# Gates of a block: first two outputs interleaved, six PSUM buffers, later dhid loads, sums and norm rows tied behind products

## The chip, the cores and the metric

The kernel runs on one core of one Trainium2 chip. The metric is the device time of one execution in microseconds, the median of several runs.

## The reference, cut to what matters

One inference step of a decoder trunk (one layer, D_MODEL 1024, D_FF 2816): 1024 prompt tokens and 8 x 4 sample tokens, 1056 columns in all. Two mixers and an output projection come first; the change lies behind them, in the last two lines of the layer and the end of the feed-forward part:

```
up = rmsnorm(x, g_ffn) @ w_up;  conv = causal depthwise conv of up, width 3, with a carried buffer
a, v = split(conv);             f = (gelu(a) * v) @ w_down        # the hidden row is called dhid below
x = x + f
x = x + sigmoid(rmsnorm(x, g_ple) @ w_ple_gate) * (p @ w_ple_proj)
return x, ..., new_buf           # new_buf: the last up rows, outputs conv_prompt and conv_sample
```

## The kernel before, in words

Every float32 product is made from operands split into a high part (an ACT cast to fp32r) and a low part (a subtraction on DVE or POOL): `split`, lines 82 and 83. `mm3` (L85 to L88) issues three matmuls for one product: high x high, high x low, low x high.

The program's tail works on columns. The 1056 columns are three blocks of 352. In a block, eight **down outputs** of 128 channels are summed over the 22 tiles of the hidden row dhid (66 matmuls each, six weight groups of up to four tiles, in PSUM buffers "pd"); then eight **gate outputs** are summed over the eight tiles of the new x (24 matmuls each, two weight groups, PSUM buffers "pu").

- **Down output** (`down_out`): DVE adds the PSUM result to x (`xb`), ACT scales it into gg (high), DVE makes gg's low part, ACT squares it, and POOL, for the last output DVE, adds the square to `sqb`. The gate products read all eight gg.
- **Sums and rows**: `sums` contracts sqb with ones on TensorE (three matmuls), DVE makes the reciprocal root in some twelve tiny steps (L99 to L113); `rows` transposes it on TensorE (L2217) and DVE copies it to `rb` (L2218).
- **rest(o)**: y = gate sum x rb (DVE), sigmoid (ACT), x pe (DVE), + xb (DVE). **out_turn(o)** transposes y on TensorE (L2241), ACT copies and stores it.
- **Weights**: w_down and w_ple_gate tiles and the blocks of dhid come through one ring of five buffers `raw`, loaded by SP in a fixed sequence (`raw_load`, `pull`, L1648 to L1664): the next load is recorded when a buffer has been consumed. Weight groups are split three groups ahead into four buffers `wx` (`dn_unit`, `ahead`), odd groups on DVE and even ones on POOL, the cast always on ACT.
- **dhid**: the next block's hidden rows, eight pieces h(0) to h(7) of up to three tiles (528 KB), are loaded into the same ring (`hid_raw`) and split (`hid_split`, tiles M) during the gates of the block before. Block 0's are split during the last up-projection pair (`last_pair`).
- **Conv rows**: `last_rows` transposes the last up rows LU (eight groups of four transposes, L2136); ACT copies and stores them. They run from the list `side`.

A scheduler at build time puts the recorded instructions of each engine into one order; each engine then works in that order and waits at semaphores. `tc.issue_after(ins)` adds to an instruction that it may not stand before `ins` on its own engine; it issues nothing. The order in which the eight gate outputs and their dhid pieces are recorded is the loop at L2254:

```
for o in range(8):
    pgs[o] = gate(o)
    if b < 2:
        hid_split(b + 1, o, V)
```

Of the kernel before, what the change touches and what calls it, by code (L numbers as in the profile page):

```python
# [21 lines left out]
BLK = T // 3  # L22
# [33 lines left out]
def body(tc, I, O):  # L56
# [8 lines left out]
    with ctx:  # L65
# [19 lines left out]
        def mm3(out, lh, ll, rh, rl, start, stop_):  # L85
            PE.matmul(out, lh, rh, start=start, stop=False)  # L86
            PE.matmul(out, lh, rl, start=False, stop=False)  # L87
            PE.matmul(out, ll, rh, start=False, stop=stop_)  # L88

# [1606 lines left out]
        for b in range(3):  # L1696
            kgs = [(o, kg) for o in range(8) for kg in range(6)]
            if b == 0:
                kgs = [(o, kg) for q in (range(4), (4, 5)) for o in range(2) for kg in q] + kgs[12:]
            units += [("d", o, kg) for o, kg in kgs] + [("g", o, kg) for o in range(8) for kg in range(2)]  # L1700

        for b in range(3):
# [9 lines left out]
            for o in range(8):  # L1712
                raw_load(("g", o), k8(), w_pg[:, :, cols_(o)])
                if b < 2:
                    hid_raw(b + 1, o)

# [387 lines left out]
        def last_pair(m):  # L2104
            if m in ORDER[:6]:
                g = ORDER.index(m)
                hid_split(0, g, V if g % 2 else G)
            if m == 4:
                hid_split(0, 6, V)
# [3 lines left out]
        while post:  # L2113
            step()
        hid_split(0, 7, V)
        pX.close()
# [16 lines left out]
        def last_rows(q):  # L2133
            pt = ps.tile([128, 512], F32, name="pt")
            for j in range(4):
                PE.transpose(pt[:18, j * 128:(j + 1) * 128], LU[:, q + j], ident)  # L2136
            lo_ = p2.tile([18, 512], F32, name="lo_", bufs=1)
            A.copy(lo_, pt[:18])
            A.dma_start(cvp[:, q * 128:(q + 4) * 128], lo_[0:2])
            A.dma_start(cvs[:, q * 128:(q + 4) * 128], lo_[2:18])  # L2140

        side = [lambda q=q: last_rows(q) for q in range(0, NH2, 4)]

        def block(b):
# [10 lines left out]
            def p_in(o):  # L2155
                pe[o] = btile("pe", 3)
                SP.dma_start(pe[o], dpp[cols_(o), c])

            def down_group(pd, kg):
                wt = wq.pop(0)  # L2160
                ahead()
                for k in range(4 * kg, min(4 * kg + 4, NH)):
                    mm3(pd, wt[:, 0, k % 4], wt[:, 1, k % 4], hp_[k][0], hp_[k][1], k == 0, k == NH - 1)

# [27 lines left out]
            if b == 0:  # L2192
                for kgs in (range(4), (4, 5)):
                    for o in range(2):
                        down(o, kgs)
            for o in range(2 if b == 0 else 0, 8):
                down(o, range(6))
                for _ in range(3):
                    if side:
                        side.pop(0)()  # L2200

# [17 lines left out]

            def gate(o):  # L2220
                pg_ = psu.tile([128, BLK], F32, name="pu")
                for kg in range(2):
                    wt = wq.pop(0)
                    ahead()
                    for k in range(4 * kg, 4 * kg + 4):
                        mm3(pg_, wt[:, 0, k % 4], wt[:, 1, k % 4], GG[k][:, 0], GG[k][:, 1], k == 0, k == 7)
                return pg_

            def rest(o, pg_):
                y = Y[o] = btile("y", 3)  # L2230
                V.tensor_tensor(y, pg_, rb, OP.mult)
# [18 lines left out]

            pgs = {}
            p_in(0)
            p_in(1)
            for o in range(8):  # L2254
                pgs[o] = gate(o)
                if b < 2:
                    hid_split(b + 1, o, V)
                if o == 0:
                    rst = sums()
                    continue  # L2260
                if o == 1:
                    rows(rst)
                    rest(0, pgs.pop(0))
                rest(o, pgs.pop(o))
                if o < 7:
                    p_in(o + 1)
                out_turn(o - 1)
            out_turn(7)
# [44 lines left out]
```

## Time and profile before

| | |
|---|---|
| runs | 2036.23, 2048.02, 2044.82 us, median 2044.82 |
| profiled execution | 2045.7 us, its span 2043.8 us |
| TensorE busy | 1947.7 us, 95% of the span |
| VectorE (DVE), ScalarE (ACT), GpSimd (POOL) busy | 1247.0, 915.6, 878.2 us |
| mean granted TensorE clock | 0.974 |
| the tail that the change touches | from some 1640 us to the end |

The span is that of the profiled execution on its core; the execution's own time has 1.9 us around it. A busy share is an average over stages: in the down products TensorE is busy almost all of the time, in the gates less. What a change in the gates is worth is read from the waits there.

### The profile page before, as it was taken

What the parts mean: (1) busy time and instruction counts of PE and PEld (TensorE: products, weight loads), DVE (VectorE), ACT (ScalarE), POOL (GpSimd) and SP (SyncE); (2) the same over time, 40 slices, a digit from 0 to 9 for tenths busy, and PEclk for the clock granted to TensorE, in tenths of its full rate; (3) what the DMA queues carried; (4) which work ended last, traced back from release to release, by engine and by line L of the source; (5) the groups of instructions that cost most, each with busy time, mean ns of one, the idle gap of its engine ahead of it and who ended that gap; (6) DMA issues with size and microseconds to landing.
All of it is one profiled execution on the core that took longest, in us unless ns stands there. A gap on an engine that the chain in (4) does not pass through costs nothing.

```text
span 2043.8 us, 35840 instructions
## 1 busy us (share of the span) xinstructions
PE 1947.7 (95%) x13329; PEld 1832.4 (90%) x13329; DVE 1247.0 (61%) x2451; ACT 915.6 (45%) x1910; POOL 878.2 (43%) x934
## 2 busy tenths in 40 slices
PE   7998999999999989999999899999999999899998
PEld 6897888888787778888999899999999989899998
DVE  5518533245778856665554877878888872734524
ACT  5512332243566634555333454444444454544543
POOL 1106441102314212222432777878788854344342
PEclk9998999999999969999999999999999999999999
DMA  7402221244322100004465422222222274755743
GB/s 242 137 11 65 67 62 51 69 124 137 87 58 58 32 1 12 2 1 151 132 179 183 130 98 90 69 81 77 72 87 66 92 234 136 229 176 175 224 143 99
DMA packets 291927, 211.53 MB, mean 103 GB/s; under 512 B 38417, under 2 KB 273092, under 8 KB 291754
## 3 DMA queue, kind: packets, MB, share of 16 engines
q1 hardware_dynamic: 275102, 195.86, 32.2%
q10 hardware_dynamic: 16652, 13.39, 2.1%
q8 instruction: 105, 1.72, 0.4%
q14 instruction: 68, 0.56, 0.1%
HBM read 161.07 MB, written 46.78 MB: 102 GB/s over the span
## 4 chain that ended last, share of the span: by engine, by line
PE 73%; DVE 10%; POOL 2%; ACT 2%; DMA 2%; issue 2%; SPq 1%; ACTq 0%; DVEq 0%; POOLq 0%
PE q L2023 21%; PE pd L87 4%; PE pd L86 4%; PE pd L88 4%; PE q L1950 3%; PE pm L88 3%; PE pm L87 3%; PE pm L86 3%; PE pv L1382 3%; PE pt L86 2%; PE pt L87 2%; PE pt L88 2%; PE p L86 2%; PE p L88 2%; PE p L87 1%
## 5 line engine op out<-in xcount | busy, mean ns | idle before, releaser
L2023 PE MATMUL q<-M,wx 128*128 128x264 f32 x2112 | 280.8, 286 | 2.0 <-DVE up L2043 2.0
L2023 PEld LDWEIGHTS q<-M,wx 128*128 128x128 f32 x2112 | 268.1, 189 | 2.3 <-issue 2.1
L83 POOL TENSOR_TENSOR wx<-raw,wx 128x512 fp32r<-128x512 f32 x108 | 146.3, 1356 | 228.2 <-ACT wx L82 222.0
L82 ACT CAST wx<-raw 128x512 fp32r<-128x512 f32 x226 | 133.4, 597 | 194.9 <-PE pd L88 114.4
L2023 PE MATMUL q<-P,wx 128*128 128x264 f32 x1584 | 216.2, 286 | 0.1
L2023 PEld LDWEIGHTS q<-P,wx 128*128 128x128 f32 x1584 | 200.6, 188 | 3.8 <-DVE up L2035 3.8
L83 DVE TENSOR_TENSOR wx<-raw,wx 128x512 fp32r<-128x512 f32 (+1 forms) x118 | 91.4, 776 | 141.6 <-ACT wx L82 138.2
L86 PE MATMUL pd<-M,wx 128*128 128x352 f32 x528 | 171.6, 325 | 0.0
L88 PE MATMUL pd<-M,wx 128*128 128x352 f32 x528 | 171.1, 324 | 0.0
L87 PE MATMUL pd<-M,wx 128*128 128x352 f32 x528 | 171.1, 324 | 0.0
L2066 DVE SCALAR_TENSOR_TENSOR cv<-up,cw,cv 128x1024 f32<-128x1024 f32 x88 | 143.2, 1627 | 28.3 <-ACT cv L2058 28.3
L88 PE MATMUL pm<-xh,wl 128*128 128x352 f32 x384 | 127.0, 331 | 0.0
L87 PE MATMUL pm<-xl,wh 128*128 128x352 f32 x384 | 126.5, 329 | 0.0
L86 PE MATMUL pm<-xh,wh 128*128 128x352 f32 x384 | 126.4, 329 | 0.0
L1756 ACT CAST wx<-raw 128x512 fp32r<-128x512 f32 x110 | 67.9, 618 | 71.9 <-PE q L2023 47.1
L86 PEld LDWEIGHTS pd<-M,wx 128*128 128x128 f32 x528 | 99.8, 189 | 0.1
L87 PEld LDWEIGHTS pd<-M,wx 128*128 128x128 f32 x528 | 99.7, 189 | 0.0
L88 PEld LDWEIGHTS pd<-M,wx 128*128 128x128 f32 x528 | 99.6, 189 | 0.1
L1364 POOL TENSOR_TENSOR Pt<-Pt,mstT 128x128 f32<-128x128 f32 x64 | 30.8, 484 | 160.1 <-ACT Pt L1363 160.1
L1950 PE MATMUL q<-M,wx 128*128 128x264 f32 x720 | 92.0, 289 | 4.1 <-POOL wx L83 2.6
L1950 PEld LDWEIGHTS q<-M,wx 128*128 128x128 f32 x720 | 89.8, 191 | 5.3 <-POOL wx L83 3.1
L83 POOL TENSOR_TENSOR wl<-wst,wh 128x1024 fp32r<-128x1024 f32 x16 | 39.3, 2456 | 104.2 <-ACT wh L82 100.1
(706 smaller groups left out, 5480.6 us busy)
## 6 DMA issues: line engine op xcount, KB each, us to landing
raw<-w_down SPq DMA_DIRECT2D x48, 512.0 KB
raw<-w_up SPq DMA_DIRECT2D x44, 512.0 KB
raw<-w_ple_gate SPq DMA_DIRECT2D x24, 512.0 KB
dhid<-cv SPq DMA_DIRECT2D x22, 528.0 KB
raw<-dhid SPq DMA_DIRECT2D x21, 528.0 KB
raw<-w_down SPq DMA_DIRECT2D x24, 384.0 KB
wst<-w_in SPq DMA_DIRECT2D x16, 512.0 KB
cb<-cache_ckv SPq DMA_DIRECT2D x64, 128.0 KB
```

The source lines that it names most:

```text
L82: A.copy(hi, src)
L83: (eng or G).tensor_tensor(lo, src, hi.bitcast(F32), OP.subtract)
L86: PE.matmul(out, lh, rh, start=start, stop=False)
L87: PE.matmul(out, lh, rl, start=False, stop=False)
L88: PE.matmul(out, ll, rh, start=False, stop=stop_)
L1364: masked[0] = G.tensor_tensor(Pt[:, :128], Pt[:, :128], mstT, OP.add)
L1382: PE.matmul(W["pv"][:, j, :DV + 1], Pts[k][:, q0:q0 + 128], Vb[hp][:, k, e], start=k == 0, stop=k == i)
L1756: A.copy(w[:, 0], s)
L1950: PE.matmul(p_[:, n, :QW], a_, b_[:, k % 4], start=k + x == 0 and kg == 0, stop=k == 7 and x == 2)
L2023: PE.matmul(o_, l_, r_, start=start and k + x == 0, stop=k + x == 5, skip_group_check=not start)
L2066: V.scalar_tensor_tensor(C[:, :S], U[:, tp:tp + S], w[tp], C[:, :S], op0=OP.mult, op1=OP.add)
```

## The change

In words: (1) `mm3` returns its last matmul, so that others can be tied behind it. (2) The first two gate outputs are computed together, weight group by weight group. (3) Gate outputs 3 to 5 use the three "pd" buffers, which makes six PSUM buffers. (4) h(0) is loaded behind g(3), h(1) to h(3) behind g(4) to g(6), h(4) to h(7) behind g(7); the splits of the pieces are recorded from gate 3 on. (5) `sums` is tied behind the first two outputs (48 matmuls), `rows` behind the third (72). (6) The transposes of outputs are recorded later and left to the scheduler. (7) The conv rows run two per down output behind its products, with two copies' buffers, not three before them. (8) The last piece of block 0's dhid is split behind the first four groups of outputs 0 and 1. (9) "pe" and "y" have four buffers.

```diff
@@ -85,7 +85,7 @@
         def mm3(out, lh, ll, rh, rl, start, stop_):
             PE.matmul(out, lh, rh, start=start, stop=False)
             PE.matmul(out, lh, rl, start=False, stop=False)
-            PE.matmul(out, ll, rh, start=False, stop=stop_)
+            return PE.matmul(out, ll, rh, start=False, stop=stop_)
 
         def mm2(out, l2, rh, rl, start, stop_):
 
@@ -1697,7 +1697,7 @@
             kgs = [(o, kg) for o in range(8) for kg in range(6)]
             if b == 0:
                 kgs = [(o, kg) for q in (range(4), (4, 5)) for o in range(2) for kg in q] + kgs[12:]
-            units += [("d", o, kg) for o, kg in kgs] + [("g", o, kg) for o in range(8) for kg in range(2)]
+            units += [("d", o, kg) for o, kg in kgs] + [("g", o, kg) for op in ((0, 1), (2,), (3,), (4,), (5,), (6,), (7,)) for kg in range(2) for o in op]
 
         for b in range(3):
             if b == 0:
@@ -1711,8 +1711,9 @@
                     dn_load(o, i)
             for o in range(8):
                 raw_load(("g", o), k8(), w_pg[:, :, cols_(o)])
-                if b < 2:
-                    hid_raw(b + 1, o)
+                for g in {7: (4, 5, 6, 7)}.get(o, (o - 3,) if o > 2 else ()):
+                    if b < 2:
+                        hid_raw(b + 1, g)
 
         wsum = {}
 
@@ -2105,14 +2106,13 @@
             if m in ORDER[:6]:
                 g = ORDER.index(m)
                 hid_split(0, g, V if g % 2 else G)
-            if m == 4:
+            if m == 3:
                 hid_split(0, 6, V)
 
         for j in range(NH):
             up_pair(j, first_pair if j == 0 else last_pair if j == NH - 1 else lambda m: None)
         while post:
             step()
-        hid_split(0, 7, V)
         pX.close()
         f1.close()
 
@@ -2134,12 +2134,14 @@
             pt = ps.tile([128, 512], F32, name="pt")
             for j in range(4):
                 PE.transpose(pt[:18, j * 128:(j + 1) * 128], LU[:, q + j], ident)
-            lo_ = p2.tile([18, 512], F32, name="lo_", bufs=1)
+            lo_ = p2.tile([18, 512], F32, name="lo_", bufs=2)
             A.copy(lo_, pt[:18])
             A.dma_start(cvp[:, q * 128:(q + 4) * 128], lo_[0:2])
             A.dma_start(cvs[:, q * 128:(q + 4) * 128], lo_[2:18])
 
         side = [lambda q=q: last_rows(q) for q in range(0, NH2, 4)]
+
+        pe_ = [None]
 
         def block(b):
             c0 = b * BLK
@@ -2153,14 +2155,14 @@
                 SP.dma_start(xb[o], dx2[cols_(o), c])
 
             def p_in(o):
-                pe[o] = btile("pe", 3)
+                pe[o] = btile("pe", 4)
                 SP.dma_start(pe[o], dpp[cols_(o), c])
 
             def down_group(pd, kg):
                 wt = wq.pop(0)
                 ahead()
                 for k in range(4 * kg, min(4 * kg + 4, NH)):
-                    mm3(pd, wt[:, 0, k % 4], wt[:, 1, k % 4], hp_[k][0], hp_[k][1], k == 0, k == NH - 1)
+                    pe_[0] = mm3(pd, wt[:, 0, k % 4], wt[:, 1, k % 4], hp_[k][0], hp_[k][1], k == 0, k == NH - 1)
 
             def down_out(o, pd):
                 V.tensor_tensor(xb[o], pd, xb[o], OP.add)
@@ -2193,11 +2195,14 @@
                 for kgs in (range(4), (4, 5)):
                     for o in range(2):
                         down(o, kgs)
+                    if 0 in kgs:
+                        hid_split(0, 7, V)
             for o in range(2 if b == 0 else 0, 8):
                 down(o, range(6))
-                for _ in range(3):
+                for _ in range(2):
                     if side:
-                        side.pop(0)()
+                        with tc.issue_after(pe_[0].ins):
+                            side.pop(0)()
 
             def sums():
                 pss = ps.tile([128, 512], F32, name="pt")
@@ -2217,17 +2222,25 @@
                     PE.transpose(pt[:, t0:t0 + n], rst[:n, i:i + 1].to_broadcast([n, 128]), ident[:n, :n])
                 V.tensor_copy(rb, pt[:, :BLK])
 
-            def gate(o):
-                pg_ = psu.tile([128, BLK], F32, name="pu")
+            pgs = {}
+
+            def gate(os_):
+                for o in os_:
+                    pgs[o] = psd.tile([128, BLK], F32, name="pd") if 2 < o < 6 else psu.tile([128, BLK], F32, name="pu")
                 for kg in range(2):
-                    wt = wq.pop(0)
-                    ahead()
-                    for k in range(4 * kg, 4 * kg + 4):
-                        mm3(pg_, wt[:, 0, k % 4], wt[:, 1, k % 4], GG[k][:, 0], GG[k][:, 1], k == 0, k == 7)
-                return pg_
+                    for o in os_:
+                        wt = wq.pop(0)
+                        ahead()
+                        for k in range(4 * kg, 4 * kg + 4):
+                            pe_[0] = mm3(pgs[o], wt[:, 0, k % 4], wt[:, 1, k % 4], GG[k][:, 0], GG[k][:, 1], k == 0, k == 7)
+
+            def held(f, *a):
+
+                with tc.issue_after(pe_[0].ins):
+                    return f(*a)
 
             def rest(o, pg_):
-                y = Y[o] = btile("y", 3)
+                y = Y[o] = btile("y", 4)
                 V.tensor_tensor(y, pg_, rb, OP.mult)
                 A.activation(y, y, AF.Sigmoid)
                 V.tensor_tensor(y, pe[o], y, OP.mult)
@@ -2248,23 +2261,29 @@
                 if m < 96:
                     A.dma_start(ysv[:, oc], yo[m:96, 2])
 
-            pgs = {}
+            def rows_in(g):
+                if b < 2:
+                    hid_split(b + 1, g, V)
+
             p_in(0)
             p_in(1)
-            for o in range(8):
-                pgs[o] = gate(o)
-                if b < 2:
-                    hid_split(b + 1, o, V)
-                if o == 0:
-                    rst = sums()
-                    continue
-                if o == 1:
-                    rows(rst)
-                    rest(0, pgs.pop(0))
+            p_in(2)
+            gate((0, 1))
+            rst = held(sums)
+            gate((2,))
+            held(rows, rst)
+            for o in range(3):
                 rest(o, pgs.pop(o))
-                if o < 7:
-                    p_in(o + 1)
-                out_turn(o - 1)
+            for o in range(3, 8):
+                p_in(o)
+                gate((o,))
+                rest(o, pgs.pop(o))
+                rows_in(o - 3)
+                for j in {3: (0,), 4: (1, 2), 5: (3, 4)}.get(o, (o - 1,)):
+                    out_turn(j)
+            rows_in(5)
+            rows_in(6)
+            rows_in(7)
             out_turn(7)
 
         for b in range(3):
```

What the build makes of it, at three places. Names: M are split dhid tiles, wx split weight groups, raw the ring's buffers; the number after a name tells buffers apart.

**DVE, where the down products begin.** Before (up: evacuations of the last up-projection, cv: convolution steps):

```order
L2050 TENSOR_TENSOR up_18937<-q_18987,up_18937 128x2x264
L83 TENSOR_TENSOR M1_19164<-raw_19065,M0_19163 128x1056
L2066 SCALAR_TENSOR_TENSOR cv_19174<-up_18937,cw_11337,cv_19174 128x1024
L83 TENSOR_TENSOR M5_19170<-raw_19096,M4_19169 128x1056
L2066 SCALAR_TENSOR_TENSOR cv_19174<-up_18937,cw_11337,cv_19174 128x1024
L2073 TENSOR_TENSOR up_18936<-q_19098,up_18936 128x2x264
L83 TENSOR_TENSOR wx_19258<-raw_19020,wx_19258 128x512
L2066 SCALAR_TENSOR_TENSOR cv_19173<-up_18936,cw_11337,cv_19173 128x1024
```

and now:

```order
L2051 TENSOR_TENSOR up_18937<-q_18987,up_18937 128x2x264
L83 TENSOR_TENSOR M1_19164<-raw_19065,M0_19163 128x1056
L2067 SCALAR_TENSOR_TENSOR cv_19170<-up_18937,cw_11337,cv_19170 128x1024
L2074 TENSOR_TENSOR up_18936<-q_19098,up_18936 128x2x264
L2067 SCALAR_TENSOR_TENSOR cv_19170<-up_18937,cw_11337,cv_19170 128x1024
L83 TENSOR_TENSOR M5_19211<-raw_19096,M4_19210 128x1056
L2067 SCALAR_TENSOR_TENSOR cv_19169<-up_18936,cw_11337,cv_19169 128x1024
L2068 SCALAR_TENSOR_TENSOR cv_19169<-ub0_19215,cw_11337,cv_19169 128x32
L2067 SCALAR_TENSOR_TENSOR cv_19169<-up_18936,cw_11337,cv_19169 128x1024
L2068 SCALAR_TENSOR_TENSOR cv_19169<-ub0_19215,cw_11337,cv_19169 128x32
L83 TENSOR_TENSOR wx_19252<-raw_19020,wx_19252 128x512
```

The split of the fourth weight group from raw_19020 stood behind one convolution (cv_19174); now it stands behind both.

**DVE, from the last down output's add to the first gate outputs of block 0.** Before:

```order
L83 TENSOR_TENSOR M7_20188<-raw_19990,M6_20187 128x1056
L83 TENSOR_TENSOR wx_20085<-raw_19904,wx_20085 128x256
L83 TENSOR_TENSOR M13_20249<-raw_20056,M12_20248 128x1056
L83 TENSOR_TENSOR wx_20117<-raw_19958,wx_20117 128x512
L83 TENSOR_TENSOR M9_20314<-raw_20120,M8_20313 128x1056
L2166 TENSOR_TENSOR xb_19934<-pd_20052,xb_19934 128x352
L83 TENSOR_TENSOR wx_20155<-raw_20022,wx_20155 128x512
L2170 SCALAR_TENSOR_TENSOR gg_20144<-xb_19934,gt_62,gg_20144 128x352
L2176 TENSOR_TENSOR sqb_19251<-sqb_19251,sq_20147 128x352
L83 TENSOR_TENSOR M3_20369<-raw_20191,M2_20368 128x1056
L2209 TENSOR_SCALAR msx_20197<-pt_20193 128x2
```

and further down, from the last step of the reciprocal root on:

```order
L113 SCALAR_TENSOR_TENSOR rst_20198<-rf_a_20203,rf_i_20202 128x3
L2208 MEMSET msx_22725 128x1
L83 TENSOR_TENSOR wx_20281<-raw_20158,wx_20281 128x512
L2218 COPY rb_19252<-pt_20254 128x352
L2231 TENSOR_TENSOR y_20259<-pu_20154,rb_19252 128x352
L2231 TENSOR_TENSOR y_20264<-pu_20215,rb_19252 128x352
L83 TENSOR_TENSOR M1_20479<-raw_20317,M0_20478 128x1056
L2231 TENSOR_TENSOR y_20319<-pu_20280,rb_19252 128x352
L2233 TENSOR_TENSOR y_20259<-pe_20150,y_20259 128x352
```

and now:

```order
L83 TENSOR_TENSOR wx_20076<-raw_19877,wx_20076 128x256
L83 TENSOR_TENSOR wx_20108<-raw_19963,wx_20108 128x512
L2168 TENSOR_TENSOR xb_19907<-pd_20043,xb_19907 128x352
L83 TENSOR_TENSOR wx_20158<-raw_19963,wx_20158 128x512
L2172 SCALAR_TENSOR_TENSOR gg_20135<-xb_19907,gt_62,gg_20135 128x352
L2178 TENSOR_TENSOR sqb_19245<-sqb_19245,sq_20138 128x352
L83 TENSOR_TENSOR M7_20338<-raw_20079,M6_20337 128x1056
L83 TENSOR_TENSOR wx_20190<-raw_19995,wx_20190 128x512
L2214 TENSOR_SCALAR msx_20226<-pt_20222 128x2
L2215 TENSOR_SCALAR msx_20226<-pt_20222 96x1
```

and further down:

```order
L113 SCALAR_TENSOR_TENSOR rst_20227<-rf_a_20232,rf_i_20231 128x3
L2213 MEMSET msx_22760 128x1
L83 TENSOR_TENSOR M13_20393<-raw_20161,M12_20392 128x1056
L2223 COPY rb_19246<-pt_20277 128x352
L83 TENSOR_TENSOR wx_20300<-raw_20126,wx_20300 128x512
L2244 TENSOR_TENSOR y_20282<-pu_20156,rb_19246 128x352
L2244 TENSOR_TENSOR y_20287<-pu_20157,rb_19246 128x352
L2244 TENSOR_TENSOR y_20292<-pu_20244,rb_19246 128x352
L83 TENSOR_TENSOR M9_20457<-raw_20248,M8_20456 128x1056
L2246 TENSOR_TENSOR y_20282<-pe_20150,y_20282 128x352
L2246 TENSOR_TENSOR y_20287<-pe_20152,y_20287 128x352
L2247 TENSOR_TENSOR y_20282<-y_20282,xb_19247 128x352
```

Three dhid splits (M7, M13, M9) stood before or among the steps up to the add of xb; now the first stands behind sqb, the second between the norm's last step (rst) and the copy rb, the third between the y multiplications and the pe multiplications.

**SP, the loads of block 0's gates, and ACT, the first weight group of block 1.** Before:

```order
L1664 DMA raw_19904<-w_down 128x6x128
L1664 DMA raw_19958<-w_ple_gate 128x8x128
L1664 DMA raw_19990<-dhid_73 128x3x352
L1664 DMA raw_20022<-w_ple_gate 128x8x128
L1664 DMA raw_20056<-dhid_73 128x3x352
L1664 DMA raw_20088<-w_ple_gate 128x8x128
L1664 DMA raw_20120<-dhid_73 128x3x352
L1664 DMA raw_20158<-w_ple_gate 128x8x128
L1664 DMA raw_20191<-dhid_73 128x3x352
L1664 DMA raw_20219<-w_ple_gate 128x8x128
L1664 DMA raw_20252<-dhid_73 128x3x352
```

and on ACT:

```order
L2244 DMA y_prompt<-yo_20495 128x2x128
L2245 COPY yo_20495<-pt_20491 96x128
L2247 DMA y_prompt<-yo_20495 96x128
L82 CAST wx_20518<-raw_20449 128x512
L82 CAST wx_20556<-raw_20449 128x512
```

and now:

```order
L1664 DMA raw_19877<-w_down 128x6x128
L1664 DMA raw_19931<-w_ple_gate 128x8x128
L1664 DMA raw_19963<-w_ple_gate 128x8x128
L1664 DMA raw_19995<-w_ple_gate 128x8x128
L1664 DMA raw_20047<-w_ple_gate 128x8x128
L1664 DMA raw_20079<-dhid_73 128x3x352
L1664 DMA raw_20126<-w_ple_gate 128x8x128
L1664 DMA raw_20161<-dhid_73 128x3x352
L1664 DMA raw_20193<-w_ple_gate 128x8x128
L1664 DMA raw_20248<-dhid_73 128x3x352
L1664 DMA raw_20303<-w_ple_gate 128x8x128
L1664 DMA raw_20341<-dhid_73 128x3x352
```

and on ACT:

```order
L2258 COPY yo_20475<-pt_20471 96x128
L82 CAST wx_20500<-raw_18806 128x512
L2260 DMA y_prompt<-yo_20475 96x128
L82 CAST M14_20575<-raw_20396 128x1056
L2245 ACTIVATE y_20515<-y_20515 128x352
```

The dhid loads alternated with the gate loads from the first one on; now four gate loads stand together, and dhid follows. Block 1's first weight group was read from a new load (raw_20449); now it is read from raw_18806, the tile that block 0's first group was read from.

## Rows read from the trace of the kernel before

**Rows 1.** The page: busy us, share of the span and instructions.
```profile
PE 1947.7 (95%) x13329; PEld 1832.4 (90%) x13329; DVE 1247.0 (61%) x2451; ACT 915.6 (45%) x1910; POOL 878.2 (43%) x934
```

**Rows 2.** What TensorE waited for, 1620 to 2044 us: total us, times, longest.
```profile
PE pt L2241 <- DVE y L2234: 5.4, 5, 2.1
PE pt L2136 <- ACT lo__19560 L2138: 2.9, 1, 2.9
PE pt L2205 <- DVE sqb L2176: 2.1, 2, 1.0
```

**Rows 3.** Tile pu, blocks 0, 1, 2: min/median/max ns, first and last start.
```profile
L88 PE MATMUL pu<-gg,wx x64: 318/322/496, 1749.4 to 1791.0; 128*128 128x352 f32 x64
...
L88 PE MATMUL pu<-gg,wx x64: 318/323/496, 1876.8 to 1916.0; 128*128 128x352 f32 x64
...
L88 PE MATMUL pu<-gg,wx x64: 317/322/327, 2001.9 to 2036.5; 128*128 128x352 f32 x64
```

**Rows 4.** Chain of waits in block 2's gates: start us, us, what.
```profile
2002.37 0.16 PE pu L87
...
2005.58 0.51 PE pt L2205 x6
...
2020.07 0.33 PE pt L2241 x3
```

**Rows 5.** Chain of waits in block 0's gates.
```profile
1744.27 5.48 DMA raw<-dhid
...
1752.05 0.52 DVE xb L2166
...
1753.90 4.83 DMA raw<-dhid
...
1771.04 0.52 PE pt L2241 x3
...
1771.74 0.29 PE pu L87
...
1774.73 0.29 PE pu L86
```

**Rows 6.** Groups of ACT, DVE, POOL, 1749 to 1800 us: busy, mean ns | idle before.
```profile
L82 ACT CAST wx<-raw 128x512 fp32r<-128x512 f32 x21 | 12.7, 617 | 10.0 <-PE pu L88 4.6 <-ACT yo L2245 1.7 <-DMA xb<-dx 1.6
L82 ACT CAST M<-raw 128x1056 fp32r<-128x1056 f32 x5 | 5.4, 1074 | 7.9 <-DMA raw<-dhid 7.9
...
L2232 ACT ACT_TABLE_LOAD x1 | 1.3, 1283 | 0.0
...
L83 DVE TENSOR_TENSOR wx<-raw,wx 128x512 fp32r<-128x512 f32 x9 | 6.8, 758 | 1.3 <-ACT wx L82 1.0
L83 DVE TENSOR_TENSOR M<-raw,M 128x1056 fp32r<-128x1056 f32 x5 | 6.3, 1253 | 3.2 <-ACT M L82 3.2
L2233 DVE TENSOR_TENSOR y<-pe,y 128x352 f32<-128x352 f32 x8 | 5.2, 657 | 0.6 <-ACT y L2232 0.6
...
L83 POOL TENSOR_TENSOR wx<-raw,wx 128x512 fp32r<-128x512 f32 x11 | 15.4, 1397 | 36.6 <-ACT wx L82 36.6
```

**Rows 7.** Busy time by stretch, block 0's gates: length, engines, PEclk, DMA share, GB/s.
```profile
1748.80:1791.00 42.20, 36.80 (x221) 35.12 (x220) 30.41 (x53) 23.57 (x45) 12.33 (x9) 0.96 0.84 246
```

**Rows 8.** Chain of waits where the down products begin.
```profile
1654.77 0.70 DVE up L2050
...
1658.75 0.90 PE pt L2136 x4
1659.65 0.29 PE pd L86
```

**Rows 9.** Tile cv on DVE, 1652 to 1672 us: min/median/max ns.
```profile
L2066 DVE SCALAR_TENSOR_TENSOR cv<-up,cw,cv x4: 1272/1280/2337, 1657.1 to 1664.0; 128x1024 f32<-128x1024 f32 x4
```

**Rows 10.** Chain of waits in the last up-projection pair.
```profile
1638.61 3.81 DMA raw<-dhid
```

**Rows 11.** Tile rst in block 2's gates.
```profile
L113 DVE SCALAR_TENSOR_TENSOR rst<-rf_a,rf_i x1: 161/161/161, 2008.8 to 2008.8; 128x3 f32<-128x3 f32 x1
```

## Prediction

> **What bounds the kernel now.** I read the busy times first: TensorE works 1947.7 us of the span of 2043.8 [rows 1], so time is won only where it stands still or runs slowly. Then the table of its waits in the part that the change moves, from 1620 us on [rows 2]: the largest are 5.4 us before the transposes of outputs, 2.9 before the conv transposes, 2.1 before the sums. None is a wait for a free PSUM buffer. Next the three stretches of 192 gate products. From the start of the third product to that of the last it is 41.6 us in block 0, 39.2 in block 1, 34.6 in block 2 [rows 3]. At 0.16 us a product, with sums of 0.51, six output turns of 0.33 and norm rows, three transposes like a turn [rows 4], 190 products take 30.5 + 0.8 + 2.0 = 33.3. The blocks lose 8.3, 5.9 and 1.3 us: 15.5 is all that the gates can give.
>
> Why blocks 0 and 1 lose more stands in the chain of waits [rows 5]: a dhid load of 5.48 us, the ACT cast that begins its split (1.07 [rows 6]), and only then, at 1752.05, the add of the last down output, some 3 us after its product; then a load of 4.83. ACT waited 7.9 us for dhid in these gates [rows 6]. Block 2 splits no dhid. TensorE's clock falls too: after the output turn at 1771.04, ten products from 1771.74 to 1774.73 take 0.29 instead of 0.16 us [rows 5], the pace of 1.2 GHz, not 2.4; the stretch has a granted clock of 0.96 [rows 7].
>
> **The change, part by part.** Sums are against the profiled execution, 2045.7 us, the span and 1.9 around it; that is 0.9 above the median of 2044.82. Half a per cent, about what a measurement of this kernel can tell from no change, is 10.2 us.
>
> *Six PSUM buffers, four y and pe buffers, ties, the returned product:* 0. Rows 2 holds no wait for them, and a tie issues nothing.
>
> *Start of the down products.* Before, the third group of conv transposes waits 2.9 us for a copy and takes 0.90 instead of some 0.35, and ten products follow at 0.29 [rows 2, 8]: 2.9 + 0.55 + 10 x 0.13 = 4.75 lost. Now products begin with the evacuation that ends at 1654.77 + 0.70 = 1655.47 [rows 8]; the transposes cost the same later. But the split of d(0)'s fourth group, which stood behind one convolution on DVE, stands behind both: two dhid splits of 1.25, four convolution steps of 1.28, an evacuation of 0.70 and the split (0.76) [rows 6, 8, 9] make 9.1: 1664.6. TensorE has done its 36 products by 1661.3, waits 3.3, and ten slow products cost 1.3: 4.6. I take 0; the ends are 4.7 won (no wait) and 1.5 lost (the small steps between, and a later start).
>
> *Gates of blocks 0 and 1.* Count from the end of the last down product (t = 0). No dhid split stands before the add now, so add (0.52), scaled copy and subtraction (under 0.6 each by the pace of the add) give the last gg by t = 2.5. With two outputs interleaved it is wanted at product 33, t = 5.3: the waits for gg and sqb go.
>
> The dhid loads now follow the loads of later gates, and with that comes a new wait. Since h(4) to h(7) are loaded before the next block's first w_down tile, that block's first split is recorded on the old tile raw_18806 (the fence on ACT): it stays occupied, and four raw buffers rotate, not five. So h(0) takes the buffer of g(0), free when POOL has split its second half: down group 4 ends at t = -1.0, cast 0.6, POOL 1.4 [rows 6], load at t = 1.0. Loads beside other loads landed in 4.83 to 5.48 us [rows 5], one almost alone in 3.81 [rows 10]. I take 4.9, nearest to the case with one gate load beside it. Landed at 5.9, cast by 7.0, split by 8.3; behind it on DVE a weight split (0.76) and the norm chain, which took 2.9 in block 2 (sums end at 2006.09, last step 2008.8 + 0.16 [rows 4, 11]): 12.0. TensorE wants the norm rows after 72 products, sums and, in block 0, four conv transposes: t = 12.5, in block 1 12.0. No wait.
>
> h(1) takes h(0)'s buffer: issued at 8.4, landed 13.3, cast by 14.4 with weight casts queued behind on ACT, split by 15.7, ahead of the rb copy that every y needs. Copy (0.52 like the add), a weight split (0.76) and three y multiplications (0.52 each): 18.5. h(2)'s split is next: 19.8; the sigmoid table (1.28 [rows 6]) and three sigmoids on ACT run meanwhile. Two pe multiplications and y(0)'s addition, 0.66 each [rows 6]: y(0) at 21.8. TensorE wants it 33 products behind the norm rows in block 0 (t = 18.1) and 31 in block 1 (17.3): it waits 3.7 and 4.5, and ten slow products and a slow turn cost 1.6. Block 0 loses 5.3 instead of 8.3, block 1 6.1 instead of 5.9: **3.0 won, 0.2 lost.** The bounds: all 8.3 + 5.9 won, and landings of 5.5 (the last rival).
>
> The row says 4.83 to 5.48 for 528 KB. The Trainium skill (DMA: Bandwidth & Descriptors, Anatomy of one DMA) fits one transfer of the GpSimd path by 2.0 us plus bytes over 436 GB/s: 3.2 us for it, an estimate that no row here reaches. By it, both chained loads together would land 3.4 us earlier and y(0)'s wait would all but go.
>
> *Start of the next block.* Its first group reads the kept tile. The second needs a load that goes after POOL's split in gate 7 (t = 35.3; the gates end at 39.4) and is split by 41.5, when the 12 products of the first end (41.3): 0. Output 1's first load waits for h(6)'s split (43.1) and is split by 50.3, wanted at 50: hidden by output 0's 66 products. If that cover goes, it costs two to three us a block.
>
> *Block 2* has no dhid. Rows at 11.9, y(0) ready some 4 us later, wanted 26 products behind, 16.4: the 1.3 is won. The closing chain from the last product to the last store is unchanged.
>
> **Sum:** 0 - 3.0 + 0.2 - 1.3 = -4.1, so 2041.6 us; I give 2042.
>
> **Rivals.** *Shorter landings*, 3.8 us each [rows 10]: y(0) at 19.5, block 0 loses 3.0, block 1 3.8. Won: 5.3 + 2.1 + 1.3 = 8.7, so 2037.0. For it: fewer loads are in flight at once. Against: the engines' DMA share is 0.84 in these gates [rows 7], and the same bytes move in less time.
>
> *All waits go*: no split stands in the way and the down start is won, 8.3 + 5.9 + 1.3 + 4.7 = 20.2: 2025.5. For it: block 2 runs nearly so. Against: rows 5 shows DVE's add held by a dhid split ahead of it, and such splits now stand ahead of rb and the pe multiplications.
>
> *Slower: the dhid chain reaches into the next block.* With landings of 5.5 us block 0 loses 6.5 and block 1 7.3 (with block 2, 1.7 won in all); h(6)'s split then ends after t = 44, the point from which TensorE waits for output 1's weights: 2.2 us and 1.3 of slow clock at both block starts, 7.0; the down start loses 1.5. 2045.7 - 1.7 + 7.0 + 1.5 = 2052.5. For it: three of the four links are loads whose slot is freed by the link before. Against: 4.83 was also seen.
>
> *It moves nothing*, y(0)'s new wait being as long as the old ones in block 0 too: 2045, the upper part of the forecast's own case.
>
> **How the numbers follow.** Forecast 0.44 (by itself 2036 to 2047), shorter landings 0.24, all waits go 0.12, slower 0.20. Faster by over 0.5% (below 2034.6): all of the third, 0.4 of the second, a tenth of the first, 0.26. Slower (above 2055.0): half of the last, whose price could double, 0.10. Within: 0.64. The range 2030 to 2053 leaves out the third case and part of the last, some 0.2.
>
> **What would show it.** Right: the waits for gg and before the conv transposes gone; a wait of 3 to 5 us of the first L2254 transposes for a y addition in blocks 0 and 1, and in the chain there a dhid load, its cast and its split ahead of the rb copy; gate stretches near 39, 39 and 33 us; a wait for a weight split near 1661. Wrong: y(0) in time in both blocks (the second or third case), or TensorE waiting for weights or dhid splits in the first 12 us of blocks 1 and 2 (the slower one).

## The result: slower by about half a per cent

| | before | after |
|---|---|---|
| median, runs | 2042.14 us, 13 | 2054.42 us, 13 |
| profiled execution, its span | 2045.7, 2043.8 us | 2053.07, 2051.3 us |
| mean granted TensorE clock | 0.974 | 0.973 |

The ratio is 1.0053, 95% interval 1.004 to 1.0066. Run again on another chip, the changed kernel took 1.0043 times the kernel before, 1.0027 to 1.0059. Both intervals lie above 1: the kernel is slower, by about half a per cent. One of the 13 runs after, 2133.49 us at a granted clock of 0.839, was slow; it counts in the median and not in the ratio. The median lies 1.4 us above the forecast range of 2030 to 2053.

The part of the program ahead of the change starts the tail anywhere from 1641.5 to 1654.6 us in the traces of this study, so spans are no measure of ten microseconds. I compare lengths of stages inside each trace, from the start times of TensorE's products. "Start 0" runs from the 25th matmul from the end of the up-projection to the first gate product of block 0, so it holds the start of the down products and block 0's down products. "Gates" runs from the first to the last of a block's 192 gate products. "Start 1" and "start 2" run from a block's last gate product to the next block's first one. "Tail" runs from the beginning of start 0 to the end of the span. Stages in us, ratios to runs of the kernel before on the same chip:

| kernel | start 0 | gates 0 | start 1 | gates 1 | start 2 | gates 2 | tail | ratio, 95% interval |
|---|---|---|---|---|---|---|---|---|
| before | 97.6 | 41.9 | 85.5 | 39.5 | 85.5 | 34.9 | 392.3 | |
| after | 99.0 | 37.5 | 93.7 | 40.0 | 87.9 | 34.6 | 400.0 | 1.0053, 1.004 to 1.0066 |
| e5, after again | 100.4 | 38.4 | 94.7 | 38.9 | 89.6 | 34.6 | 404.0 | 1.0043, 1.0027 to 1.0059 |
| e1, first w_down tile early | 99.9 | 38.9 | 87.4 | 39.3 | 88.2 | 34.6 | 395.7 | 1.0016, 1.0003 to 1.0028 |
| e2, six yo | 99.2 | 38.2 | 93.0 | 39.8 | 89.0 | 34.6 | 401.1 | 1.0044, 1.0031 to 1.0058 |
| e3, dhid as before | 100.0 | 35.8 | 87.6 | 41.7 | 86.8 | 34.6 | 393.8 | 1.0015, 1.0002 to 1.0028 |
| e4, down start as before | 97.5 | 37.6 | 94.2 | 39.0 | 90.1 | 34.6 | 400.3 | 1.0034, 1.0018 to 1.0049 |
| e6, e1 and e4 | 96.6 | 40.9 | 87.8 | 38.8 | 90.1 | 34.6 | 396.1 | 1.0017, 1.0002 to 1.0033 |
| e7, e3 and e4 | 98.8 | 40.2 | 87.5 | 42.2 | 86.9 | 34.6 | 397.4 | 1.0031, 1.0014 to 1.0047 |
| e8, e3 with ties | 100.7 | 36.3 | 88.0 | 41.6 | 85.5 | 34.6 | 394.1 | 1.0003, 0.9987 to 1.0019 |
| e9, before with late dhid | 97.9 | 37.3 | 92.1 | 41.4 | 86.7 | 34.9 | 397.6 | 1.003, 1.0015 to 1.0045 |
| e10, e9 with the tile early | 97.9 | 39.7 | 87.4 | 38.5 | 86.3 | 34.9 | 392.1 | 1.0009, 0.9994 to 1.0023 |

Two traces of the changed kernel differ by up to 1.7 us in a stage, so smaller differences of single stages decide nothing here. After against before: block 0's gates won 4.4; the starts lost 1.4, 8.2 and 2.4. The two traced executions differ by 7.4 us, and the stages cover that. By the ratio the kernels differ by some 11 us, by the medians by 12.3, so 3 to 5 us of the difference lie outside what these two traces show and are not explained here.

### The profile page after: what moved, and what is told of

Same layout as the page of the kernel before. It is cut to its first block, busy times and chain, and to the rows that moved or that the text cites. A ratio compares the mean times of both kernels' runs of the same rounds, so it can differ in the third digit from the quotient of the medians.

```text
span 2051.3 us, 35803 instructions
## 1 busy us (share of the span) xinstructions
PE 1948.9 (95%) x13329; PEld 1833.8 (89%) x13329; DVE 1237.5 (60%) x2451; ACT 916.0 (45%) x1910; POOL 877.9 (43%) x934
## 4 chain that ended last, share of the span: by engine, by line
PE 76%; DVE 11%; DMA 5%; ACT 3%; POOL 3%; issue 3%; SPq 1%; ACTq 0%; DVEq 0%; POOLq 0%
PE q L2024 21%; PE pm L87 4%; PE pd L88 4%; PE pd L87 4%; PE pm L88 4%; PE pd L86 4%; PE pm L86 4%; PE q L1951 3%; PE pv L1382 3%; PE pt L86 2%; PE pt L87 2%; PE pt L88 2%; PE p L86 2%; PE p L88 1%; PE p L87 1%
## 5 line engine op out<-in xcount | busy, mean ns | idle before, releaser
L83 DVE TENSOR_TENSOR wx<-raw,wx 128x512 fp32r<-128x512 f32 (+1 forms) x118 | 89.6, 761 | 156.0 <-ACT wx L82 152.9
L1758 DVE TENSOR_TENSOR wx<-raw,wx 128x512 fp32r<-128x512 f32 x66 | 76.8, 1164 | 11.8 <-ACT wx L1757 11.8
```

The costliest lines, as they stand in the source:

```text
L83: (eng or G).tensor_tensor(lo, src, hi.bitcast(F32), OP.subtract)
L1758: (G if m in (2, 5, 4) else V).tensor_tensor(w[:, 1], s, w[:, 0].bitcast(F32), OP.subtract)
```

## The profile after

The page, busy time by engine. TensorE's, 1947.7 before [rows 1], is almost the same:

```profile
PE 1948.9 (95%) x13329; PEld 1833.8 (89%) x13329; DVE 1237.5 (60%) x2451; ACT 916.0 (45%) x1910; POOL 877.9 (43%) x934
```

What TensorE waited for, 1620 to 2052 us (total us, times, longest), answers to [rows 2]. The waits for the conv copy and for sqb are gone; waits for weight casts and a weight split are new, and y waits have grown from 5.4 us:

```profile
PE pt L2254 <- DVE y L2247: 11.9, 8, 3.3
PE pd L86 <- ACT wx L82: 3.8, 3, 1.8
PE pd L88 <- DVE wx L83: 3.8, 1, 3.8
```

SP's timeline where block 0's gates end (start us, us, what); before, the first w_down load of block 1:

```profile
1777.85 3.05 SPq L1664 DMA_DIRECT2D raw<-w_down  x2
```

and after, with the last two of the four dhid loads ahead of it:

```profile
1782.51 0.90 SPq L1664 DMA_DIRECT2D raw<-dhid  x2
...
1787.62 2.14 SPq L1664 DMA_DIRECT2D raw<-w_down  x2
```

Block 1's products begin at 1791.41 before and at 1789.23 after (below), so the first load's lead has shrunk from 13.6 to 1.6 us. After, the block's first weight group comes from the kept tile, so that load is wanted for the second group, 12 products of 0.16 us later: 3.5 us for a load whose cast began 5.0 us after it was issued. What that does shows on ACT after (the bracket is the idle time ahead and what ended it):

```profile
1792.60 0.62 ACT L82 CAST wx<-raw 128x512 fp32r<-128x512 f32 x1 [2.53 <-DMA raw<-w_down]
...
1796.08 0.62 ACT L82 CAST wx<-raw 128x512 fp32r<-128x512 f32 x1 [1.45 <-DMA raw<-w_down]
...
1796.60 0.49 ACT L2245 ACTIVATE y<-y 128x352 f32<-128x352 f32 x1
```

and on TensorE after:

```profile
1788.96 0.52 PE L2254 MATMUL pt<-ident,y 128*128 128x128 f32 x3 [0.87 <-DVE y L2247]
1789.23 0.41 PE L86 MATMUL pd<-M,wx 128*128 128x352 f32 x1
...
1793.27 0.44 PE L86 MATMUL pd<-M,wx 128*128 128x352 f32 x1 [1.85 <-ACT wx L82]
...
1796.75 0.43 PE L86 MATMUL pd<-M,wx 128*128 128x352 f32 x1 [0.87 <-ACT wx L82]
```

Two weight groups are late, and the last y, which needs no weight, is held behind both. On DVE its multiplication stands behind the split of the first late group:

```profile
1793.25 0.69 DVE L83 TENSOR_TENSOR wx<-raw,wx 128x512 fp32r<-128x512 f32 x1 [1.89 <-ACT wx L82]
1793.86 0.52 DVE L2244 TENSOR_TENSOR y<-pu,rb 128x352 f32<-128x352 f32 x1
```

and on ACT its sigmoid stands behind the second late cast. The chain of waits after, over block 0's gates and block 1's start, goes on from there:

```profile
1751.25 4.08 DMA raw<-dhid
...
1757.75 3.56 DMA raw<-dhid
...
1789.37 6.63 DMA raw<-w_down
...
1796.60 0.50 ACT y L2245
...
1797.13 1.31 DVE y L2246
...
1798.46 0.54 DVE y L2247
...
1799.13 0.87 PE pt L2254 x3
1800.00 0.29 PE pd L87
...
1802.35 0.26 PE pd L86
1802.61 0.16 PE pd L87
```

So the start of block 1 pays four times: 2.7 us for the casts, 2.8 for y turns (two, the longest 2.0), the slow turn at 1799.13 (0.87 instead of 0.33 [rows 4]) and nine products at 0.29: 2.7 + 2.8 + 0.5 + 9 x 0.13 = 7.2 of the 8.2. Before, TensorE waits for nothing there. The first of the two y waits, 0.87, comes before any weight is late: that y, of the last output but one, stands on DVE behind a dhid split (1786.36) that waited 2.73 us for its cast.

The clock shows in the busy times by stretch after (length, PE, PEld, DVE, ACT, POOL, granted clock, DMA share, GB/s): 0.58 of full speed, near the lower of the two levels (1.2 of 2.4 GHz), behind the wait at the down start, 0.59 behind the last y turn, full speed later:

```profile
1662.00:1666.00 4.00, 0.52 (x3) 0.52 (x4) 4.00 (x7) 1.14 (x2) 1.58 (x2) 0.99 0.96 299
1666.00:1670.00 4.00, 4.00 (x17) 4.00 (x16) 1.93 (x3) 1.07 (x2) 1.85 (x1) 0.58 0.99 336
...
1800.00:1803.00 3.00, 3.00 (x14) 3.00 (x13) 1.53 (x2) 0.94 (x3) 0.56 (x1) 0.59 0.73 209
1803.00:1810.00 7.00, 7.00 (x46) 7.00 (x45) 2.69 (x4) 3.67 (x7) 2.58 (x2) 1.00 0.92 264
```

## The experiments

My theory: four dhid loads now stand ahead of the next block's first w_down load in the ring, and the late load costs the block start. Rivals: the output stores hold SP, or the interleaved outputs and later turns are at fault. Diffs are against the changed kernel unless another is named.

**e1**, the first w_down tile of the next block is loaded ahead of h(4) to h(7), and not again later:

```diff
                     if b < 2:
+                        if g == 4:
+                            dn_load(0, 0)
                         hid_raw(b + 1, g)
```

> The changed kernel with one load moved: the next block's first w_down tile is loaded ahead of dhid pieces 4 to 7, not behind them. Its first weight group is then read from the new tile, and five raw buffers rotate again. Theory A (the ring: the late first w_down load behind four dhid loads, with one raw buffer kept occupied, makes TensorE wait at the start of blocks 1 and 2, 7.1 and 1.8 us more than before): the starts fall to under 1 us lost each, the time by 7 to 9 us against the changed kernel, and y(0) in the gates comes some 1 us earlier or stays. Theory B (the load waits for stores of y, since three yo buffers and their queue hold ACT and SP): the load still lands late, gain under 3 us. Theory C (DVE and ACT are blocked by the dhid splits that now fall at the block's end): the wait moves from weights to h(5) to h(7), gain 2 to 4 us.

Block 1's start fell from 93.7 to 87.4. The ratio's interval lies below that of the changed kernel and below that of e2, run on the same chip; it touches the lower end of e5's. The loss of under 1 us at each start that was expected was not reached: block 1's start stays 1.9 us above before, and block 2's, 88.2, did not move by more than the scatter. Not all was won in the gates either: TensorE now waits at the norm rows, where it did not in the changed kernel (waits of e1, 1620 to 2052 us):

```profile
PE pt L2225 <- DVE msx L2216: 3.5, 1, 3.5
PE pt L2225 <- DVE rst L113: 3.4, 1, 3.4
```

With the new tile loaded early, the kept one should come free and five buffers rotate. The trace fits that: the first dhid load goes at 1744.55, not at 1751.25 as in the changed kernel, and more dhid splits stand on DVE in front of the norm chain. The chain of waits of e1 in block 0 shows two of them ahead of the last step of the root:

```profile
1752.84 5.39 DMA raw<-dhid
...
1759.35 1.26 DVE M L83
...
1764.46 1.26 DVE M L83
...
1766.22 0.16 DVE rst L113
```

**e2**, the stores:

```diff
-                yo = p2.tile([128, 3, 128], F32, name="yo", bufs=3)
+                yo = p2.tile([128, 3, 128], F32, name="yo", bufs=6)
```

> The changed kernel with six yo buffers for the transposed outputs instead of three. Theory B: ACT's wait of 2.4 us for a store goes, the w_down load of block 1 is issued some 5 us earlier, and the time falls by 4 to 7 us. Theory A: ACT's wait goes, but the load still waits for the ring and the split of the kept tile; 0 to 2 us.

Nothing moved: start 1 is 93.0 and the ratio 1.0044. But the wait that the edit was to take away did not go either, against both theories: ACT still waits 2.5 us for a store of y (2.4 in the changed kernel), and in both traces the second w_down load of block 1 goes out just as a store has landed (1789.31 and 1789.37 in the changed kernel, 1793.17 and 1793.23 here). So the number of yo buffers is no cause; what the stores themselves cost is not shown by this run.

**e3**, dhid loaded and split gate by gate again, the rest of the change kept:

```diff
-                for g in {7: (4, 5, 6, 7)}.get(o, (o - 3,) if o > 2 else ()):
-                    if b < 2:
-                        hid_raw(b + 1, g)
+                if b < 2:
+                    hid_raw(b + 1, o)
...
             gate((0, 1))
+            rows_in(0)
+            rows_in(1)
             rst = held(sums)
             gate((2,))
+            rows_in(2)
...
-                rows_in(o - 3)
+                rows_in(o)
...
-            rows_in(5)
-            rows_in(6)
-            rows_in(7)
```

> The changed kernel with the loads and splits of the next block's dhid as before the change: piece g loaded behind gate weight g and split behind gate g. The interleaved outputs, the six PSUM buffers, the ties and the conv rows stay. Theories A and C alike: the block starts lose as little as before the change (0.3 us each), some 9 us less than now. For the gates: if the early splits alone caused the old waits for gg and sums, block 0 and 1 lose about 8 and 6 us again, 2 us net worse than now, and the time is 6 to 8 us under the changed kernel; if interleaving covers them (gg wanted at product 33 instead of 21), they lose 3 to 5 each and the time is 9 to 12 us under it, and so at or under the kernel before.

The ratio is 1.0015, some 6 us under e2 on the same chip. Start 1 is 87.6 and start 2 86.8, shorter by 6.1 and 1.1 but not as short as before. Block 0's gates keep their gain, 35.8. Block 1's take 41.7: the norm rows wait there 3.1 us for the reciprocal root, and its chain shows a dhid load of 6.29 us in front of the root's steps:

```profile
1878.16 6.29 DMA raw<-dhid
...
1884.48 1.08 ACT M L82
...
1886.76 1.24 DVE rf_i L100
...
1890.06 0.17 DVE rst L113
```

**e4**, the down start as before (the last split of block 0's dhid ahead of the products, conv rows untied and three at a time):

```diff
-            if m == 3:
+            if m == 4:
                 hid_split(0, 6, V)
...
+        hid_split(0, 7, V)
...
-                    if 0 in kgs:
-                        hid_split(0, 7, V)
...
-                for _ in range(2):
+                for _ in range(3):
                     if side:
-                        with tc.issue_after(pe_[0].ins):
-                            side.pop(0)()
+                        side.pop(0)()
```

> The changed kernel with the start of the down products as before: pieces 6 and 7 of block 0's dhid split at their old places, and three groups of conv rows ahead of the products, not tied. If the split of the fourth weight group behind both convolutions costs what the trace shows (6.3 us lost there against 4.8 before), the time falls by 1 to 2 us against the changed kernel; if the conv rows between the products cost something too, by up to 3. The gates and the block starts stay as they are.

Start 0 went back to 97.5, that of before, and the old wait with it (2.8 us for a conv copy). The time, 1.0034, is not told apart from that of e2 on the same chip, 1.0044. Over all traces, start 0 is 97.7 on average with the old down start (six kernels) and 99.7 with the new one (five, e8 apart): the new one loses some 2 us. The edit puts back the order of the splits and the conv rows together, so it does not tell which of them costs that.

**e5**, the changed kernel once more, as a base on the second chip:

> The changed kernel once more, beside the next three on one chip, to have its distance to the kernel before and to them from the same chip. Every theory: 1.003 to 1.007 times the kernel before. Where the ratio falls near the lower end, the sum of the stages in the traces (7 us) is the whole effect; near the upper end some 4 us more would be outside the stages that the traces compare.

The ratio, 1.0043, lies between the two ends and decides for neither.

**e6**, e1 and e4 together:

> The changed kernel with both repairs: the next block's first w_down tile loaded ahead of dhid pieces 4 to 7, and the start of the down products as before. If the two causes (late w_down with an occupied ring buffer; the split behind both convolutions) add, some 9 to 11 us under the changed kernel, 0.998 to 1.001 of the kernel before. If the first repair only moved the wait into the gates (3.5 us before the norm rows in its trace), the gain over that repair alone stays under 1 us.

1.0017: no better than e1. What start 0 won, 3.3 us against e1, came back in block 0's gates, 40.9, where the norm rows wait 4.5 us (3.5 in e1), and in start 2, 90.1.

**e7**, e3 and e4 together, so that interleaving, six PSUM buffers, the ties and the y and pe buffers remain:

> The changed kernel with loads and splits of dhid and the start of the down products as before: what is left of the change is the interleaving of the first two outputs, six PSUM buffers, more y and pe buffers, the ties of sums and norm rows, and the transposes left to the scheduler. If the forecast was right that these win in block 0's gates and little elsewhere, the ratio to the kernel before is 0.997 to 1.000. If the interleaving itself costs (norm rows tied behind 72 products wait 3.1 us in block 1), 1.000 to 1.002.

1.0031: what remains does not pay either. The waits for gg and sqb stay gone, but the old one for the conv copy is back, longer, and the norm rows wait (waits of e7, 1620 us to the end):

```profile
PE pt L2136 <- ACT lo__19560 L2138: 4.5, 1, 4.5
PE pt L2219 <- DVE rst L113: 3.7, 1, 3.7
PE pt L2219 <- DVE msx L2210: 3.1, 1, 3.1
```

As from e1 to e6, block 0's gates are longer with the old down start: 40.2, against 35.8 in e3. Why is open.

**e8**, e3, with the dhid splits from h(2) on tied behind the copy to rb, the last convolution recorded behind the first down group, and piece 6 of block 0's dhid split at its old place (parts of the edit):

```diff
...
+                down(0, (0,))
+                while post:
+                    step()
+                down(0, (1, 2, 3))
+                down(1, range(4))
+                hid_split(0, 7, V)
+                for o in range(2):
+                    down(o, (4, 5))
...
-                rows_in(o - 3)
+                with tc.issue_after(rb_[0].ins):
+                    rows_in(o)
```

> The changed kernel with dhid loads as before, splits of dhid pieces 2 to 7 tied on DVE behind the copy of the norm rows, and the last up-projection's convolution recorded behind the first down group, with the conv rows between the products as in the change. If DVE's order is what holds TensorE at all three places (split of a weight group behind two convolutions, norm chain behind dhid splits), the down start loses under 1.5 us instead of 6.3, the norm rows do not wait, and the ratio is 0.993 to 0.997. If the dhid splits put off then hold the next block's start, 0.997 to 1.002 and a wait for weights or M there.

1.0003: the same as before, by the interval, where 0.993 to 0.997 was expected. The norm rows wait less (1.3 us), but start 0 is 100.7: the one wait of 3.8 for a weight split became several for later groups, 1.9 and 0.9 for splits and 1.2 for a cast.

The last two take the theory out of the changed kernel. **e9** is the kernel before with the late dhid alone:

```diff
-                if b < 2:
-                    hid_raw(b + 1, o)
+                for g in {7: (4, 5, 6, 7)}.get(o, (o - 3,) if o > 2 else ()):
+                    if b < 2:
+                        hid_raw(b + 1, g)
...
                 pgs[o] = gate(o)
-                if b < 2:
-                    hid_split(b + 1, o, V)
+                for g in {7: (4, 5, 6, 7)}.get(o, (o - 3,) if o > 2 else ()):
+                    if b < 2:
+                        hid_split(b + 1, g, V)
```

> The kernel before with part (4) of the change alone: h(0) loaded and split from gate 3 on, h(4) to h(7) loaded behind g(7), ahead of the next block's first w_down tile. Nothing else is changed. Theory A (the late first w_down load is the cause of the loss, and it needs no other part of the change): the starts of blocks 1 and 2 grow as in the changed kernel, from 85.5 to 91 to 95 us in block 1 and to 87 to 89 in block 2, with TensorE waiting for the cast or split of the block's first weight group; block 0's gates fall from 41.9 to 37 to 39 us, since no dhid split stands before the last down output's add; sum 3 to 9 us more than before. Theory B (the loss needs the interleaved outputs or the later output turns): the block starts stay within 2 us of 85.5 and the time within 3 us of before.

The time is 1.003 times before, start 1 is 92.1 and gates 0 37.3: the gain, 4.6 us, and most of the loss, 6.6 of 8.2, come with the dhid order alone. Neither the interleaved outputs nor the later turns are needed for them, and the stores are those of the kernel before. The wait is not where I expected it, though: 0.2 us for the weight cast, 4.5 for y turns. The chain of e9 shows the same cause one step on, the last y held by the late weights. Its multiplication stands on DVE (1791.63) behind the split of the first late group, which waited 1.76 us for its cast, and its sigmoid behind the next cast, which waits for w_down:

```profile
1785.82 6.27 DMA raw<-w_down
...
1792.17 0.04 ACT wx L82
...
1792.70 0.51 ACT y L2233
...
1793.23 1.29 DVE y L2234
...
1796.30 0.88 PE pt L2242 x3
```

**e10** is e9 with the first w_down tile loaded ahead of h(4) to h(7), by e1's edit:

> The run before, and the next block's first w_down tile is loaded ahead of h(4) to h(7). Theory A: the wait for the block's first weight group is gone, block 1's start is 85 to 88 us, block 0's gates stay at 37 to 39, and the time is 0 to 5 us below the kernel before: only the gates' gain is left. Theory B: no difference to the run with the late dhid alone. If theory A holds for the starts but the time is no better than before, a new wait (the norm rows behind a dhid split, as in the changed kernel with this load early) has taken what the gates gain.

Start 1 fell to 87.4, and TensorE waits for no weight there. On the same chip the median is 2046.15 against e9's 2050.58. The tail, 392.1, is that of before, and the ratio's interval holds 1: gates 0 and 1 won 2.2 and 1.0, starts 1 and 2 lost 1.9 and 0.8, the smaller of them within the scatter. No run was faster than the kernel before.

**Still open:** start 2. The changed kernel waits there for a cast, 1.1 us, 1.6 in e5 and 2.2 in e4. In e1 and e6 that wait is gone, but a last y turn waits 0.9 and 2.2 behind an ACT cast instead, and the stage is no shorter. What would free that turn was not tried. Start 1, too, stays some 2 us longer than before where its weights are early: TensorE waits there for the last y turns, 1.7 us in e1, 2.1 in e3 and 1.9 in e10. In e10 the last y's multiplication on DVE (1787.59) stands behind the last dhid split (1786.34); no run took that split away.

## Why the prediction was wrong

| step | forecast | measured, by stage |
|---|---|---|
| start of the down products | 0 (4.7 won to 1.5 lost) | 1.4 lost |
| gates of block 0 | 3.0 won | 4.4 won |
| start of block 1 | 0 | 8.2 lost |
| gates of block 1 | 0.2 lost | 0.5 lost |
| start of block 2 | 0 | 2.4 lost |
| gates of block 2 | 1.3 won | 0.3 won |
| sum | 4.1 won | 7.8 lost |

- **Start of the next block** is the step that failed. The prediction had the load for the second group go at 35.3 us from the last down product and the split end at 41.5. POOL's split ended at 1786.70, some 36.4 us after the first gate product (1750.3). The load went out at 1787.62, some 37.3: SP had stood 2.3 us at a pe load, by the profile for a dhid landing. Its cast began at 1792.60, and TensorE, whose first 12 products were done by 1791.4, stood still for 1.85. That is the two microseconds by which a sum with no slack was off. The larger omission is what stands behind the load: a third group from the next load, which took 6.63, and the last y, its multiplication on DVE behind the late split and its sigmoid on ACT behind the late cast. The prediction asked what TensorE reads next, and not who else stands behind the waiting cast. In its sum the step stood at 0; it measured 8.2 and 2.4 lost, e1 gave back 6.3 of the 8.2 by loading the tile early, and e9 brought 6.6 with the dhid order alone.
- **The rival that went slower** had the place (weights late at both block starts) and the size, 7.0 us against 10.6, but not the way: it needed dhid landings of 5.5 and put the wait at output 1's weights. Block 0's landings were 4.08 and 3.56, shorter than the 4.9 taken, and output 0's own weights were late. Its sign, TensorE waiting for weights in the first 12 us of blocks 1 and 2, showed. One outcome cannot tell whether its chance of 0.20 was too low; the range's end, 2053, stood at its price, though the prediction said that the price could double.
- **Gates of block 0** went as said, a little better: the waits for gg, in the full table of [rows 2] 2.4 us in both blocks, and for sqb are gone. TensorE waits 1.65 us for y(0) where 3.7 was forecast, and the stretch has a granted clock of 1.00 where it was 0.96 [rows 7]. The landings, 4.08 and 3.56, are those of the rival with shorter landings, and y(0) was there some 19.7 us after the last down product, where that rival had 19.5. In **block 1** the y(0) wait is 3.3 (4.5 forecast), and 17 slow products followed it, not ten. (The ten that the prediction read in [rows 5] are nine; the eighth and the ninth have a slow output turn of 0.64 between them.) The waits for gg before:

```profile
PE pu L87 <- DVE gg L2170: 1.4, 2, 0.7
PE pu L86 <- ACT gg L2169: 1.0, 2, 0.6
```

- **Down start:** the wait for the split is there, 3.8 us where 3.3 was forecast, and the split ended at 1665.44, not 1664.6. It takes the place of the old wait, with 1.4 us more lost, at the lower bound. The chain of waits after:

```profile
1664.83 0.61 DVE wx L83
...
1665.48 0.43 PE pd L88
...
1666.10 0.29 PE pd L87
...
1669.03 0.29 PE pd L88
```

- **Gates of block 2** had little to win, and the change did not win it: TensorE waits 0.9 us there for one y addition before and 0.8 after, and otherwise works (34.19 of 35.0 us after). The 1.3 was the difference of two sums of mine; that y(0) would come in time was wrong.
- **The page weighed in the prediction:** the Trainium skill (DMA: Bandwidth & Descriptors, Anatomy of one DMA), by its fit for the GpSimd path, gave 3.2 us for a 528 KB load, an estimate. The two chained loads of block 0 came near it, 3.56 and 4.08; in block 1's gates the same loads took 4.01 and 5.65 (chain of waits after), and 512 KB loads at the start of block 1 took 6.63, and 6.27 in e9. No one figure serves here. That other loads and stores in flight make the difference is likely, but no run shows it.

## What to carry to other kernels

When a load is moved behind others in a ring, work out the lead of the next load that TensorE needs, and require slack: here a sum that closed within 0.2 us was off by two. Then list what stands behind the waiting cast on its own in-order engine; an output's multiplication and sigmoid that needed no weight cost another two, because they stood behind a late split and a late cast. Moving one split out of one chain puts it ahead of another, so price the whole round, as the norm rows of e1 and e3 show.

## What was not expected of the hardware

A wait's cost in slow products, 0.29 us or a little less, varies: nine behind the last y turn of block 0, eleven behind the 3.8 us wait at the down start, but 17 behind the 3.3 us wait for y(0) in block 1. The chain of waits after, in block 1:

```profile
1902.64 0.87 PE pt L2254 x3
1903.51 0.29 PE pd L87
...
1907.91 0.29 PE pd L87
1908.20 0.24 PE pd L88
```

The granted clock from 1903.5 to 1908.5 us is 0.52, near 1.2 of 2.4 GHz. The 1.65 us wait for y(0) in block 0 was followed by no slow product; from 1770 to 1773 us the granted clock is 1.00.
